# Half of an output projection by Strassen's seven products on two token blocks

## The chip, the cores and the metric

The kernel runs on one core of a Trainium2 chip. The metric is the device time of one launch in microseconds (us); lower is better. All of the profile's times are of one execution, counted from its first instruction.

The engines are named as the profile names them: PE (TensorE's products; PEld is its weight load), DVE (VectorE), ACT (ScalarE), POOL (GpSimd) and SP (which issues most transfers from HBM). Each engine works through its own list of instructions in order; an instruction that needs another engine's result or a free buffer waits for it at the head of its list, and everything behind it waits too.

## The reference

One layer of a hybrid encoder trunk is computed for 384 tokens: 256 of a prompt (two blocks of 128) and 128 of running streams (a third block). The part that matters here is the end of the mixer, on 2048 features:

```python
merged = (gates[:, :, 0] * br_pool + gates[:, :, 1] * br_ssd).astype(u.dtype)
out = merged @ p['w_out']                 # (384, 2048) @ (2048, 2048), float32
...
x = x + rmsnorm(m, p['g_mix_post'])
hdn = jnp.square(jax.nn.relu(rmsnorm(x, p['g_mlp_pre']) @ p['w_up'])) @ p['w_down']
x = x + rmsnorm(hdn, p['g_mlp_post'])
```

`m` is `out`. The norm of a token needs the sum of squares over all 2048 columns of its row of `out`, so nothing behind it can start for a token block before its last column block is there.

## The kernel before

Every large product is made in three passes at TensorE's full rate. An operand is split into a high part (ScalarE casts it to fp32r: `wh`, `mh`) and a low part (VectorE subtracts the high part: `wl`, `ml`), and the products high x high, high x low and low x high are added up in PSUM. So each weight tile of 128x1024 costs one ScalarE and one VectorE operation (`wsplit`, L77 and L78).

The stage before the change, `wo_units`, makes the output projection in four column blocks `nb` of 512 columns. A block has eight units `kp`; a unit loads one weight tile of 128x1024 (two k-steps of 128 features by 512 columns), splits it, and makes 2 k-steps x 3 token blocks x 3 passes = 18 products (L1082 to L1084) into three PSUM tiles `wo`, one for each token block. The stationary operand is the block's piece of `mh` or `ml` (the merged features, kept in SBUF in `ms_`), the moving one the weights. At the end of a block ScalarE squares each PSUM tile with a running sum (`wo_sums`, L1033) and VectorE multiplies it by the gain into `hm` (`wo_gain`, L1036).

Of the fourth block, the last three units are kept and worked off by token block (54 products in a row), so that the norm of token block 0 runs on VectorE and ScalarE while TensorE still multiplies for blocks 1 and 2: `wo_root` and `wo_scale` make the factor, `wo_out` (L1065) adds the scaled row to x. `transition` then turns x by TensorE transposes (`trm`, L1162) into the layout of the next product `pj_up`; filler products (`fill`, L1178 and L1180) on the first w_up tile run while it waits.

Order is set by hand. `flow` goes through a list of units: for unit i it first asks for the tile of unit i+4 (SP), then issues the products of unit i, then the splits of unit i+3 (three buffers each for `wh` and `wl`, so the split of unit i+3 waits for the products of unit i), then what follows the unit (`post`), then `work`, which takes small tasks that were put aside by `later` as far as a budget allows. Functions placed with `at` are called between two units and so stand at that place in every engine's list. `need(tag)` forces the tasks up to that tag.

The down projection further on already uses the seven-product form (`down_units`, `token_sums`, `merge`), with its token sums on VectorE and its results added up in HBM.

## Time and profile before

| | |
|---|---|
| runs | median 2798.02 us of 3 (2796.97 to 2801.68) |
| profiled execution | 2799.5 us, span from first to last instruction 2797.7 us |
| products of the output projection | 576, from 1627.7 to 1758.3 us |
| mean granted clock | 0.998 |

Rows of a profile are read so: line and engine, operation, output<-inputs by the program's names with buffer numbers left out, shape, xcount, then after the bar busy us, mean ns of one, and the engine's idle time just before them with what ended it. Matmuls overlap in the pipeline, so the time of one in a row is found from first to last start and the count, not from its duration. A window row gives, for a stretch of time, the busy time of PE, PEld, DVE, ACT and POOL with their counts, the granted clock, the share of the transfer engines' time and GB/s.

### The profile page before, as it was taken

The numbers are of one execution on the slowest core, as the hardware profiler recorded it, in microseconds if no ns is written. First come the engines' busy times: TensorE is split into PE (matmuls) and PEld (weight loads), VectorE is DVE, ScalarE is ACT, GpSimd is POOL, SyncE is SP. The second block draws the span as 40 slices with busy tenths as digits, with TensorE's granted clock in tenths as the row PEclk, the third lists the DMA queues.
The fourth block names the chain that finished last, engine by engine and source line by source line (L and its number), as shares of the span: only waits on it lengthen the run. The fifth ranks groups of instructions, "written<-read, shape, count | busy, mean of one in ns | idle before, by whom it ended". The sixth has DMA issues, their size and how long they took to land.

```text
span 2797.7 us, 40260 instructions
## 1 busy us (share of the span) xinstructions
PE 2784.7 (100%) x15964; PEld 2656.5 (95%) x15964; DVE 1766.9 (63%) x2217; ACT 1323.5 (47%) x2076; POOL 191.0 (7%) x295
## 2 busy tenths in 40 slices
PE   9999999999999999999999999999999999999998
PEld 9999999999999999999999988999999999999997
DVE  8774334567667767667633334666767667676766
ACT  6443223555555554554422223545555555555553
POOL 0000000000000000001000000000111111111111
PEclk9999999999999999999999999999999999999999
DMA  6444445556556556555744454445666566666656
GB/s 223 134 134 139 138 141 171 191 170 216 193 181 209 197 183 208 199 184 186 263 158 155 151 200 132 153 165 185 179 162 166 162 161 163 176 177 186 183 125 249
DMA packets 161468, 492.89 MB, mean 176 GB/s; under 512 B 20032, under 2 KB 43392, under 8 KB 156416
## 3 DMA queue, kind: packets, MB, share of 16 engines
q1 hardware_dynamic: 133008, 406.07, 43.1%
q0 software_dynamic: 28128, 84.24, 12.6%
q8 instruction: 125, 2.05, 0.3%
q14 instruction: 63, 0.52, 0.1%
q10 hardware_dynamic: 144, 0.01, 0.0%
HBM read 412.35 MB, written 77.89 MB: 175 GB/s over the span
## 4 chain that ended last, share of the span: by engine, by line
PE 94%; DVE 2%; DMA 1%; ACT 1%; issue 1%; SPq 0%; DVEq 0%; ACTq 0%
PE pj_up L162 6%; PE pj_up L163 6%; PE pj_up L164 6%; PE pj_x L162 4%; PE pj_x L163 4%; PE pj_x L164 4%; PE wd L1410 3%; PE pj_sp L162 3%; PE wd L1411 3%; PE wd L1412 3%; PE pj_sp L164 3%; PE pj_sp L163 3%; PE pj_z L163 3%; PE pj_z L164 3%; PE pj_z L162 3%; PE t L1412 2%
## 5 line engine op out<-in xcount | busy, mean ns | idle before, releaser
L162 PE MATMUL pj_up<-x1h,wh_up 128*128 128x384 f32 x992 | 334.6, 337 | 0.0
L163 PE MATMUL pj_up<-x1l,wh_up 128*128 128x384 f32 x992 | 333.7, 336 | 0.0
L164 PE MATMUL pj_up<-x1h,wl_up 128*128 128x384 f32 x992 | 333.7, 336 | 0.0
L162 PE MATMUL pj_x<-xgh,wh_x 128*128 128x384 f32 x768 | 257.6, 335 | 0.0
L164 PE MATMUL pj_x<-xgh,wl_x 128*128 128x384 f32 x768 | 256.9, 335 | 0.0
L163 PE MATMUL pj_x<-xgl,wh_x 128*128 128x384 f32 x768 | 256.9, 335 | 0.0
L78 DVE TENSOR_TENSOR wl_wd<-raw,wh_wd 128x1024 fp32r<-128x1024 f32 x168 | 201.8, 1223 | 62.7 <-ACT wh_wd L77 59.0
L77 ACT ACTIVATE wh_wd<-raw 128x1024 fp32r<-128x1024 f32 x168 | 174.2, 1053 | 84.5 <-PE pj_up L163 42.1
L162 PEld LDWEIGHTS pj_up<-x1h,wh_up 128*128 128x128 f32 x992 | 186.9, 188 | 4.5
L163 PEld LDWEIGHTS pj_up<-x1l,wh_up 128*128 128x128 f32 x992 | 186.9, 188 | 4.5
L164 PEld LDWEIGHTS pj_up<-x1h,wl_up 128*128 128x128 f32 x992 | 186.9, 188 | 0.0
L164 PE MATMUL pj_z<-xgh,wl_z 128*128 128x384 f32 x512 | 171.3, 335 | 0.0
L162 PE MATMUL pj_z<-xgh,wh_z 128*128 128x384 f32 x512 | 171.3, 335 | 0.0
L163 PE MATMUL pj_z<-xgl,wh_z 128*128 128x384 f32 x512 | 171.3, 335 | 0.0
L162 PE MATMUL pj_sp<-abh,wh_sp 128*128 128x384 f32 x512 | 171.2, 334 | 0.0
L164 PE MATMUL pj_sp<-abh,wl_sp 128*128 128x384 f32 x512 | 171.2, 334 | 0.0
L163 PE MATMUL pj_sp<-abl,wh_sp 128*128 128x384 f32 x512 | 171.2, 334 | 0.0
L78 DVE TENSOR_TENSOR wl_sp<-w_sp,wh_sp 128x1024 fp32r<-128x1024 f32 x64 | 78.4, 1226 | 110.7 <-ACT wh_sp L77 110.7
L162 PEld LDWEIGHTS pj_x<-xgh,wh_x 128*128 128x128 f32 x768 | 144.3, 188 | 0.0
L163 PEld LDWEIGHTS pj_x<-xgl,wh_x 128*128 128x128 f32 x768 | 144.3, 188 | 0.0
L164 PEld LDWEIGHTS pj_x<-xgh,wl_x 128*128 128x128 f32 x768 | 144.2, 188 | 0.0
L78 DVE TENSOR_TENSOR wl_x<-w_x,wh_x 128x1024 fp32r<-128x1024 f32 x72 | 87.4, 1221 | 81.3 <-ACT wh_x L77 81.3
(388 smaller groups left out, 7094.2 us busy)
## 6 DMA issues: line engine op xcount, KB each, us to landing
w_up<-w_up SPq DMA_DIRECT2D x126, 512.0 KB, 4.6
raw<-w_down SPq DMA_DIRECT2D x112, 512.0 KB, 7.1
w_x<-w_in SPq DMA_DIRECT2D x96, 512.0 KB, 4.0
w_z<-w_in SPq DMA_DIRECT2D x64, 512.0 KB, 4.5
w_sp<-w_ssd SPq DMA_DIRECT2D x64, 512.0 KB, 4.7
acc_scr<-ev POOLq DMA_DIRECT2D x126, 256.0 KB, 4.4
w_ga<-w_in SPq DMA_DIRECT2D x32, 512.0 KB, 3.4
w_pp<-w_pp SPq DMA_DIRECT2D x32, 512.0 KB, 3.4
```

Of the source, the lines that this page charges most:

```text
L77: s.activation(h, w, AF.Copy)
L78: v.tensor_tensor(l, w, h.bitcast(F32), ALU.subtract)
L162: te.matmul(out, wh, xh, start=first, stop=False)
L163: te.matmul(out, wh, xl, start=False, stop=False)
L164: return te.matmul(out, wl, xh, start=False, stop=last)
L1410: te.matmul(o, ah, wh[:, c], start=first, stop=False)
L1411: te.matmul(o, ah, wl[:, c], start=False, stop=False)
L1412: te.matmul(o, al, wh[:, c], start=False, stop=fin)
```

## The change

Columns 1024 to 2047 stay plain tiles (`wo_units(2)` and `wo_units(3)`, 16 units in all). Columns 0 to 1023 are made by `wo_pairs(c8)`, once for each half c8 of the 2048 features. For each half, the features (two groups of 512), the prompt's tokens (two blocks of 128) and the columns (two groups of 512) form a 2x2 by 2x2 block product, which takes seven products of token sums with weight sums; the third token block is multiplied plainly (tiles 7 and 8, named `wot`). Eight steps use one weight tile of 128x2048 each, in two units q; a unit makes 6 products for each of its one or two uses. Four weight tiles are loaded, and the other four steps use sums of weights that VectorE adds in place (`add`).

The token sums are made by GpSimd: `wo_tok_add` joins high and low parts of the merged features (four additions of 128x256), `wo_tok_diff` forms four sums in six operations, and `wo_tok_split` has ScalarE and VectorE split them. Results leave PSUM into nine SBUF tiles `wo_ac`: ScalarE copies those of the first half, VectorE adds those of the second. `wo_merge` puts seven operations on VectorE into the tasks, which make the four tiles of the two prompt blocks; their gain (6 products of 128x512) is made by GpSimd, in place, and their squares by ScalarE.

The order of the stage is a string. P is a plain unit; three digits are a paired unit (half c8, step j, part q); a and d are the additions and differences of tokens on GpSimd, c is their split, b is the squares and gain of the third block:

```python
    plain = wo_units(2) + wo_units(3)
    ones_ = wo_pairs(0), wo_pairs(1)
    order = "a00 d0 a01 d1 P P P c0 P 000 001 010 011 c1 a10 d0 a11 d1 020 021 030 031 P 040 041 P 050 051 P 060 061 070 071"
    order += " 100 101 c0 P 110 111 c1 120 121 130 131 P 140 141 P b0 150 b1 151 160 161 P 170 171"
```

Five plain units of the last block follow. The loads of x are put among the tasks; the first two w_up tiles are loaded when the paired units have ended (`wo_turn`) and split behind unit 6 of the last block instead of units 0 and 1; the sum over column blocks that the norm starts from (`wo_early`) comes after the merge. PSUM is given out as 2 + 2 + 4 banks instead of 4 + 4, and again as 4 + 4 in `transition`.

GpSimd's list at the start of the stage. Before, gains, x and w_up tiles are only loaded:

```order
L1028 DMA gpo0_15620<-g_mix_post 128x512
L1028 DMA gpo1_15622<-g_mix_post 128x512
L1021 DMA x1_15610<-x_tok 128x2048 x3
L1023 DMA w_x0_15618<-w_up 128x1024
L1023 DMA w_x1_15619<-w_up 128x1024
```

After the change:

```order
L1032 DMA gpo1_15632<-g_mix_post 128x512
L1157 ISA
L1157 TENSOR_TENSOR wo_t_15640<-mh0_13622,ml0_13623 128x256
L1157 TENSOR_TENSOR wo_t_15640<-mh1_13753,ml1_13754 128x256
L1157 TENSOR_TENSOR wo_t_15640<-mh4_14146,ml4_14147 128x256
L1157 TENSOR_TENSOR wo_t_15640<-mh5_14277,ml5_14278 128x256
L1171 TENSOR_TENSOR wo_sf0_15641<-wo_t_15640 128x256 x2
L1171 TENSOR_TENSOR wo_sf0_15641<-wo_sf0_15641 128x256
L1171 TENSOR_TENSOR wo_sf0_15641<-wo_t_15640 128x256 x2
L1171 TENSOR_TENSOR wo_sf0_15641<-wo_sf0_15641,wo_t_15640 128x256
```

The first ten additions stand behind the gains' loads and a row ISA; x's loads come behind the second ten.

VectorE's list at the end of a plain column block. Before, at the end of block 1 (`hm` are the gain products):

```order
L78 TENSOR_TENSOR wl_wo2_0_16003<-w_wo2_0_15934,wh_wo2_0_16002 128x1024
L78 TENSOR_TENSOR wl_wo2_1_16027<-w_wo2_1_15958,wh_wo2_1_16026 128x1024
L1036 TENSOR_TENSOR hm_15611<-wo1_0_15837,gpo1_15622 128x512
L1036 TENSOR_TENSOR hm_15611<-wo1_1_15838,gpo1_15622 128x512
L1036 TENSOR_TENSOR hm_15611<-wo1_2_15839,gpo1_15622 128x512
L78 TENSOR_TENSOR wl_wo2_2_16065<-w_wo2_2_15982,wh_wo2_2_16064 128x1024
```

After the change, at the end of block 2, which falls between the paired units 101 and 110 to 120 (`wl_wop1_2_0` is the low part of unit 120's weights, `wor` a weight tile, `wo_sl` a low part of token sums):

```order
L78 TENSOR_TENSOR wl_wop1_1_0_16127<-wor1_12_16079,wh_wop1_1_0_16126 128x1024
L1207 TENSOR_TENSOR wo_ac0_15617<-wor1_0_16095,wo_ac0_15617 128x512
L1176 TENSOR_TENSOR wo_sl_15644<-wo_sf0_15641,wo_sh_15643 128x4x256
L78 TENSOR_TENSOR wl_wop1_1_1_16153<-wor1_12_16079,wh_wop1_1_1_16152 128x1024
L1188 TENSOR_TENSOR wor1_11_16041<-wor1_11_16041,wor1_12_16079 128x2048
L1052 TENSOR_TENSOR hm0_15614<-wo2_0_15667,gpo2_15628 128x512
L1052 TENSOR_TENSOR hm1_15615<-wo2_1_15668,gpo2_15628 128x512
L1052 TENSOR_TENSOR hm2_15616<-wo2_2_15669,gpo2_15628 128x512
L78 TENSOR_TENSOR wl_wop1_2_0_16177<-wor1_21_16112,wh_wop1_2_0_16176 128x1024
```

Between two splits of weights there now stand a result from PSUM, a low part of token sums, an addition of weights and three gain products.

VectorE's list at the last unit. Before:

```order
L78 TENSOR_TENSOR wl_wo3_6_16373<-w_wo3_6_16306,wh_wo3_6_16372 128x1024
L78 TENSOR_TENSOR wl_wo3_7_16377<-w_wo3_7_16330,wh_wo3_7_16376 128x1024
L1036 TENSOR_TENSOR hm_15611<-wo3_0_16253,gpo3_16039 128x512
L1059 RECIPROCAL n2_10_16405<-n0_10_16400 128x1
L1060 TENSOR_SCALAR n1_10_16401<-n1_10_16401,n2_10_16405 128x1
```

After the change:

```order
L78 TENSOR_TENSOR wl_wo3_6_16506<-w_wo3_6_16430,wh_wo3_6_16505 128x1024
L1267 SCALAR_TENSOR_TENSOR wo_ac6_15623<-wo_ac6_15623,wo_ac4_15621 128x512
L1268 TENSOR_TENSOR wo_ac5_15622<-wo_ac5_15622,wo_ac4_15621 128x512
L78 TENSOR_TENSOR wl_wo3_7_16518<-w_wo3_7_16456,wh_wo3_7_16517 128x1024
L1269 SCALAR_TENSOR_TENSOR wo_ac2_15619<-wo_ac5_15622,wo_ac2_15619 128x512
L1062 TENSOR_TENSOR spre_16525<-st1_15626 128x3
L1063 TENSOR_TENSOR spre_16525<-spre_16525,st1_15626 128x3
L1064 TENSOR_SCALAR sneg_16526<-spre_16525 128x3
L1065 TENSOR_SCALAR spre_16525<-spre_16525 128x3
L1141 TENSOR_TENSOR wl_x0_16451<-w_x0_16448,wh_x0_16450 128x1024
L1141 TENSOR_TENSOR wl_x1_16453<-w_x1_16449,wh_x1_16452 128x1024
L1052 TENSOR_TENSOR wo_ac0_15617<-wo3_0_16268,gpo3_16166 128x512
```

The last merge, the small sums and the low parts of the two w_up tiles stand between the last split and the first gain product of the norm.

The diff, without the order string above, the loads and the PSUM lines that only follow from it:

```diff
+    def hm(b, nb):
+        return wo["ac"][(1, 2, 3, 6, 7, 8)[b * 2 + nb]] if nb < 2 else wo["hm"][b] if nb == 2 else wo["ac"][(0, 4, 5)[b]]
...
     def wo_gain(nb, b):
-        v.tensor_tensor(wo["hm"][:, b, blk(nb)], wo["o", nb][b], wo["gpo", nb], ALU.mult)
+        if nb > 1:
+            v.tensor_tensor(hm(b, nb), wo["o", nb][b], wo["gpo", nb], ALU.mult)
+        else:
+            gp.tensor_tensor(hm(b, nb), hm(b, nb), wo["gpo", nb], ALU.mult)
...
-            if nb == 3 and kp in (0, 1):
-                w = wo["raw"][kp]
-                h, l = wo["first"][kp]
-                s.activation(h, w, AF.Copy)
-                v.tensor_tensor(l, w, h.bitcast(F32), ALU.subtract)
+            if nb == 3 and kp == 5:
+                need("wo_early")
+            if nb == 3 and kp == 6:
+                for w, (h, l) in zip(wo["raw"], wo["first"]):
+                    s.activation(h, w, AF.Copy)
+                    v.tensor_tensor(l, w, h.bitcast(F32), ALU.subtract)
...
+    def wo_tok_add(c8, j):
+        for i, k in enumerate((2 * j, 2 * j + 1, 4 + 2 * j, 5 + 2 * j)):
+            h, l = (x[:, :TP].bitcast(F32) for x in ms_[c8 * 8 + k])
+            gp.tensor_tensor(wo["t32"][:, i, :], h, l, ALU.add)
+
+    def wo_tok_diff(j):
...
+        ):
+            gp.tensor_tensor(o, x, y, op)
+
+    def wo_tok_split(j):
+        ks = slice(2 * j, 2 * j + 2)
+        s.activation(wo["sh"][:, :, ks, :], wo["sf"][j], AF.Copy)
+        v.tensor_tensor(wo["sl"][:, :, ks, :], wo["sf"][j], wo["sh"][:, :, ks, :].bitcast(F32), ALU.subtract)
+
+    def wo_pairs(c8):
...
+        def add(d, n):
+            v.tensor_tensor(raw[d], raw[d], raw[n], ALU.add)
+
+        steps = [
+            ("11", True, [(0, tok(0, 0)), (7, tok(0, 2))], nothing),
+            ("12", True, [(8, tok(0, 2))], lambda: add("11", "12")),
+            ("21", True, [(1, tok(4, 0)), (7, tok(4, 2))], nothing),
+            ("22", True, [(2, sums(3)), (8, tok(4, 2))], lambda: add("12", "22")),
+            ("11", False, [(4, sums(0))], lambda: add("22", "11")),
+            ("12", False, [(6, sums(2))], lambda: add("21", "22")),
+            ("22", False, [(5, sums(1))], nothing),
+            ("21", False, [(3, tok(4, 1))], nothing),
+        ]
...
+        def evict(r, o):
+            a = wo["ac"][r]
+            if c8 == 0:
+                s.copy(a, o)
+            else:
+                v.tensor_tensor(a, o, a, ALU.add)
...
+    def wo_merge():
+        a1, a2, a3, a4, a5, a6, a7 = wo["ac"][:7]
+        tt, stt = v.tensor_tensor, v.scalar_tensor_tensor
+        parts = [
+            lambda: tt(a2, a1, a2, ALU.add),
...
+        ]
+        for i, b, nb in ((2, 0, 0), (5, 1, 0), (7, 1, 1), (10, 0, 1)):
+            parts.insert(i, lambda nb=nb, b=b: wo_part(nb, b))
+        for i, f in enumerate(parts):
+            later(0.6, None, f)
+        later(0.6, "wo_early", wo_early)
...
-    for nb in range(4):
-        items += wo_units(nb)
...
+    at(wo_turn)
+    at(wo_merge)
+    items += plain
```

More of the change, by code (lines that the diff above doesn't have):

```diff
@@ L1012, in wo_open @@
         wo["x1"] = xp.tile([P, 3, DM], F32, name="x1")
-        wo["hm"] = xp.tile([P, 3, DM], F32, name="hm")
+        wo["hm"] = [xp.tile([P, 512], F32, name=f"hm{i}") for i in range(3)]
+        wo["ac"] = [xp.tile([P, 512], F32, name=f"wo_ac{i}") for i in range(9)]
         wo["st"] = xp.tile([P, 3, 4], F32, name="st1")
         wo["st2"] = xp.tile([P, 3, 4], F32, name="st2")
-        wo["first"] = [[xp.tile([P, 1024], F32R, name=f"w{n}_x{i}") for n in "hl"] for i in range(2)]
-        wo["raw"] = [xp.tile([P, 1024], F32, name=f"w_x{i}") for i in range(2)]
@@ L1018, in wo_open @@
-        for nb in range(2):
+        for nb in (2, 0, 1):
             gain_load(nb)
         for b in range(3):
-            gp.dma_start(wo["x1"][:, b, :], io["x_tok"][b])
+            later(0.0, None, lambda b=b: gp.dma_start(wo["x1"][:, b, :], io["x_tok"][b]))
+        wo["pairs"] = ExitStack()
+        sp_ = wo["pairs"].enter_context(tc.tile_pool(name="wop", bufs=1, reuse_waits="tile"))
+        wo["rawp"] = wo["pairs"].enter_context(tc.tile_pool(name="wor", bufs=4, reuse_waits="tile"))
+        wo["t32"] = sp_.tile([P, 4, TP], F32, name="wo_t")
@@ new lines, in wo_open, with gain_load, wo_turn @@
+        wo["sf"] = [sp_.tile([P, 4, 2, P], F32, name=f"wo_sf{i}") for i in range(2)]
+        wo["sh"], wo["sl"] = (sp_.tile([P, 4, 4, P], F32R, name=f"wo_s{n}") for n in "hl")
+        for f in wo["late"]:
+            f()
+    def gain_load(nb):
+        g = wo["gpo", nb] = wo["p2"].tile([P, 512], F32, tag="gpo", name=f"gpo{nb}", bufs=3)
+        gp.dma_start(g, io["g_mix_post"][blk(nb)].partition_broadcast(P))
+    def wo_turn():
+        wo["pairs"].close()
+        xp = wo["hold"].enter_context(tc.tile_pool(name="x1p3", bufs=1, reuse_waits="tile"))
+        wo["raw"] = [xp.tile([P, 1024], F32, name=f"w_x{i}") for i in range(2)]
+        wo["first"] = [[xp.tile([P, 1024], F32R, name=f"w{n}_x{i}") for n in "hl"] for i in range(2)]
```

104 lines of the change are left out of this document (89 added, 15 removed).

## The prediction

> **What bounds the kernel now.** I read the totals first, then the waits of the stage, its products, its windows, its groups, and its last microseconds in order of time.
>
> ```profile
> span 2797.7 us, 40260 instructions
> ...
> PE 2784.7 (100%) x15964; PEld 2656.5 (95%) x15964; DVE 1766.9 (63%) x2217; ACT 1323.5 (47%) x2076; POOL 191.0 (7%) x295
> ```
>
> TensorE is busy for 2784.7 of 2797.7 us. What counts is how many products it has and whether anybody makes it wait. From 1610 to 1800 us the view of TensorE's waits has three rows:
>
> ```profile
> PE trm L1162 <- issue: 0.6, 1, 0.6
> PE pj_up L1201 <- DVE x1l L1170: 0.5, 1, 0.5
> PE trm L1162 <- DVE x L1065: 0.3, 1, 0.3
> ```
>
> All three lie behind the output projection, in the turn of x to the next layer's layout; inside the projection TensorE never waits. The products, from the view of the tile wo (count, shortest/median/longest ns, first and last start), and the windows (busy time of TensorE, weight load, DVE, ACT, POOL; granted clock; DMA):
>
> ```profile
> L1082 PE MATMUL wo<-wh_wo,mh x192: 387/389/390, 1627.7 to 1757.6; 128*128 128x512 f32 x192
> L1083 PE MATMUL wo<-wl_wo,mh x192: 388/390/397, 1627.9 to 1757.9; 128*128 128x512 f32 x192
> L1084 PE MATMUL wo<-wh_wo,ml x192: 388/390/398, 1628.2 to 1758.1; 128*128 128x512 f32 x192
> ```
>
> ```profile
> 1627.70:1758.30 130.60, 130.60 (x578) 108.10 (x577) 53.13 (x62) 46.08 (x68) 2.22 (x5) 1.00 0.49 164
> 1758.30:1764.50 6.20, 4.89 (x30) 3.88 (x29) 5.18 (x13) 3.76 (x12) 0.00 (x0) 1.00 0.00 1
> 1764.50:1768.00 3.50, 3.50 (x14) 3.40 (x13) 1.95 (x5) 0.00 (x0) 0.00 (x0) 0.51 0.00 0
> ```
>
> The 576 products start from 1627.7 to 1758.1, so one takes 130.4/575 = 0.227 us; the 390 ns is its length in the pipeline. VectorE is busy 53 of 131 us, ScalarE 46, GpSimd 2. A plain tile (18 products) lasts 4.08 us. Behind the projection the clock is granted at 0.51 for 3.5 us.
>
> **Products (the gain).** Two of the four column blocks of 512 need 3 token blocks x 16 k-steps x 2 x 3 products = 288 now. The new form has, for each half of the features, 11 uses (2+1+2+2+1+1+1+1 over the eight steps) of 4 k-steps with 3 products, 132; twice that is 264. So 24 x 0.227 = **-5.4 us**. This is all that the change can take off: 0.19%.
>
> **VectorE and ScalarE in the stage.** Prices, from the groups of 1627.7 to 1758.3 us and, for operations that only the later down projection has, of the rest of the run:
>
> ```profile
> L78 DVE TENSOR_TENSOR wl_wo<-w_wo,wh_wo 128x1024 fp32r<-128x1024 f32 x30 | 36.8, 1226 | 69.0 <-ACT wh_wo L77 69.0
> L1036 DVE TENSOR_TENSOR hm<-wo,gpo 128x512 f32<-128x512 f32 x11 | 7.6, 689 | 6.2 <-ACT q L1033 6.2
> ```
>
> ```profile
> L1358 DVE TENSOR_TENSOR raw<-raw,raw 128x2048 f32<-128x2048 f32 x56 | 127.9, 2284 | 0.0
> L1308 DVE TENSOR_TENSOR sl<-sf,sh 128x1024 fp32r<-128x1024 f32 x14 | 17.2, 1226 | 15.8 <-ACT sh L1307 15.8
> L1461 DVE TENSOR_TENSOR ac<-wd,ac 128x512 f32<-128x512 f32 x12 | 7.7, 682 | 0.0
> ```
>
> ```profile
> L77 ACT ACTIVATE wh_wo<-w_wo 128x1024 fp32r<-128x1024 f32 x30 | 31.8, 1059 | 73.1 <-PE wo L1084 71.6 <-issue 1.5
> L1033 ACT ACTIVATE q<-wo 128x512 f32<-128x512 f32 x11 | 6.6, 599 | 9.7 <-PE wo L1084 9.7
> L1033 ACT ACTIVATION_READ_ACCUMULATOR q<-wo 128x1 f32 x11 | 2.1, 194 | 0.0
> ```
>
> Sixteen more weight splits, 8 additions of weights, 4 low parts of token sums, 9 additions from PSUM and 7 merges put 16 x 1.226 + 8 x 2.284 + 4 x 1.226 + 16 x 0.69 = 53.8 us on VectorE and take away 6 gain products of 0.69. In the stretch of the paired units themselves (264 products and 7 plain tiles of 18: 390 x 0.227 = 88.5 us) VectorE has 38 splits, 8 additions, 3 low parts and 11 operations from PSUM: 46.6 + 18.3 + 3.7 + 7.6 = 76.2 us, 86%. So 12.3 us are spare on the whole, but no longer beside each unit: a unit of one use lasts 6 x 0.227 = 1.36 us, and only two units are split ahead. ScalarE (splits of 1.06 us, copies of the first half's results) has less and is no bound.
>
> The place with least cover is the end of the third plain column block, ahead of unit 120 (the order of VectorE there is shown above). TensorE then has units 110 and 111, 12 products, 2.72 us. ScalarE squares the last block (0.60 + 0.19), splits the weights (1.06), VectorE makes the low part (1.23): 3.1 us, so TensorE waits 0.4. I allow as much again for like places: **+0.8**.
>
> **The tail.** What ran early now stands in front of the norm: the two splits of the first w_up tiles, the last merge, the four sums of squares. The rows of VectorE, ScalarE and TensorE from 1747 to 1763 us, in order of time (start, duration):
>
> ```profile
> 1747.37 1.23 DVE L78 TENSOR_TENSOR wl_wo<-w_wo,wh_wo 128x1024 fp32r<-128x1024 f32 x1 [2.86 <-ACT wh_wo L77]
> 1751.08 0.69 DVE L1036 TENSOR_TENSOR hm<-wo,gpo 128x512 f32<-128x512 f32 x1 [2.48 <-ACT q L1033]
> 1752.68 0.16 DVE L1059 RECIPROCAL n<-n 128x1 f32<-128x1 f32 x1 [0.92 <-ACT n L1052]
> 1753.46 2.08 DVE L1065 SCALAR_TENSOR_TENSOR x<-hm,n,x 128x512 f32<-128x512 f32 x3
> ...
> 1757.48 2.08 DVE L1065 SCALAR_TENSOR_TENSOR x<-hm,n,x 128x512 f32<-128x512 f32 x3
> ...
> 1761.50 0.75 DVE L1065 SCALAR_TENSOR_TENSOR x<-hm,n,x 128x512 f32<-128x512 f32 x1
> ```
>
> ```profile
> 1751.06 1.28 ACT L1052 ACT_TABLE_LOAD   x1
> ```
>
> ```profile
> 1758.32 1.04 PE L1162 MATMUL trm<-cst,x 128*128 128x128 f32 x8
> 1762.36 0.63 PE L1162 MATMUL trm<-cst,x 128*128 128x128 f32 x4 [0.63 <-issue]
> ```
>
> Call 0 the start of the last 54 products (1758.3 - 54 x 0.227 = 1746.1). Now VectorE ends the last split at 2.5, idles, and ends the last x row that the turn waits for at 1762.25, that is 16.15. After the change: last split 2.5, merge 0.69 to 3.2, ScalarE's square to 4.0, VectorE's four small sums to 4.8; ScalarE's two casts run from 4.0 to 6.0, VectorE's two low parts (1.14 apart) to 7.4, its gain to 8.1. ScalarE: square to 6.8, table load to 8.1, roots to 8.4. From there the old chain: 0.78 to the first x row (9.2), three of them 2.0, gain and row 1.25, next root 0.77: the first row of block 1 is done at 13.95 where TensorE is free at 12.25; three rows, gain, row, root and the last row end at 18.0. So **+1.85** against 16.15. Only about 2.2 us of the 6 us of moved work show, since VectorE used to idle there.
>
> **GpSimd.** It gets 40 additions of 128x256 and 6 gain products of 128x512, behind a row ISA. No run here has an operation of GpSimd with inputs; its nearest rows and its last free moment:
>
> ```profile
> L499 POOL MEMSET bst<- 128x1024 f32 x1 | 1.0, 973 | 0.0
> ...
> L338 POOL MEMSET pbuf<- 128x15 f32 x2 | 0.2, 110 | 31.7 <-DVE xgl L256 31.7
> ```
>
> ```profile
> 1625.05 1.11 POOL L1028 DMA_DIRECT2D gpo<-g_mix_post  x2 [261.15 <-PE pj_sp L164]
> ```
>
> A column costs (973 - 110)/1009 = 0.86 ns to write. An addition of 256 columns is then 0.10 + 0.22 = 0.32 us if its two reads are hidden, 0.76 if reads and write go one after another. I take the middle, 0.54 (1.0 for 512 columns, 1.41 at most). ScalarE must read the first sums by 1643.4: four plain tiles end at 1644.0, unit 000 at 1646.75, and the cast of the sums (1.06) and the split behind it (1.06 + 1.23) stand ahead of unit 001. GpSimd has 1626.7 to 1643.4, 16.7 us, for ten additions (5.4, at most 7.6): cost 0, and 9 us cover the ISA row. The second ten are wanted at 1654: covered too.
>
> Whether GpSimd and VectorE hold each other up when both read SBUF no row tells. Bounds: nothing; or every GpSimd operation that meets VectorE delays it by its whole length. About 30 additions and 2 gain products fall into the stretch of 88.5 us, 18.2 us, of which 86% meet VectorE: 76.2 + 15.7 = 91.9, +3.4 over TensorE's 88.5; in the tail the four gain products stand between the merges, in front of the last split, where one of 1.0 delays TensorE directly: +1.3 with the merge that it also pushes. I take +2 of the 3.4, since operations that meet are half over on average, and the 1.3: **+3.3**. The Trainium skill's page "SBUF — State Buffer", section "Who interferes with whom", speaks against the change here: a VectorE instruction with two SBUF inputs and a GpSimd instruction that reads SBUF exclude each other, and the second waits for all of the first. By that rule the 3.4 stand in place of my 2, and the sum below would be +2.0 instead of +0.6; no run here shows it yet.
>
> **Transfers.** SP issues as many bytes; the paired halves are asked for four units ahead, 5.5 us at the tightest (unit 020 asked for at 1644.0, split at 1649.5). The weights' tiles land so (shortest, median, longest), while x's three transfers, now behind GpSimd's sums, take long:
>
> ```profile
> DMA to landing us min/median/max: 3.3/3.4/8.6
> ```
>
> ```profile
> x<-x_tok POOLq DMA_DIRECT2D x3, 1024.0 KB, 11.5
> ```
>
> At 3.4 us they are covered; 8.6 beside x's transfers would cost up to 3 us once. I take 0 and keep the 3 for the range. The first w_up tiles are wanted some 15 us after their issue: 0. PSUM's two banks for results come free one step ahead: 0.
>
> **Sum:** -5.4 + 0.8 + 1.85 + 3.3 = **+0.6 us**, on a profiled execution of 2799.5 us (span 2797.7). The median of the runs, 2798.02, is 1.5 below it; I set the sum on the median: **2798.6**. The runs spread over 2796.97 to 2801.68, so about 0.2% (5.6 us) is what can be told from no change.
>
> **Rivals.** (1) GpSimd and VectorE do not meet: -5.4 + 0.8 + 1.85 = -2.8, 2795.2. For it: the additions from PSUM and most units leave VectorE gaps; against it: 86% load. (2) Slower: GpSimd holds VectorE up, at 0.76 and 1.41 us. 0.86 x (30 x 0.76 + 2 x 1.41) = 22.0 and 76.2 + 22.0 - 88.5 = +9.7, tail +2: -2.8 + 11.7 = +8.9, 2806.9. It decides against the change (+5.6) from about 0.65 us an addition. (3) GpSimd's first sums come late: ScalarE stands at their cast with all splits behind it, and each microsecond beyond the 9 of cover is one of TensorE; at 15 us for the ISA row +6, 2804.6. The Trainium skill's page "GPSIMD Engine Reference", section 2.1, gives about 6 us for loading a kernel's code at first use, which would be covered. (4) The gain stays whole: moved work hides and the 3.5 us at clock 0.51 fall away (half of it, -1.7): 2798.0 - 5.4 - 1.7 = 2790.9.
>
> **Chances.** Forecast 0.48, (1) 0.22, (2) 0.18, (3) 0.07, (4) 0.05. Faster by over 0.2% is (4) alone, 0.05; slower by over 0.2% is (2), (3) and a little of the forecast, 0.28; within it 0.67. The range leaves out (4) and the far part of (2) and (3): 2793.5 to 2807.0.
>
> **What would show it.** TensorE's count falls by 24; the waits of TensorE name wl_wop, the low halves of the paired tiles, for 1 to 4 us in all, and wl_wo of the last tile for about 1; the first turn of x starts 1.5 us or more after the last product; GpSimd's additions show 0.5 to 0.6 us. VectorE's low parts (1226 ns) unchanged beside running additions would speak for rival 1. ScalarE waiting for the sums at their cast would speak for rival 3. A wait on w_out2's transfers, or a second stretch at half clock, would make the prediction wrong in a way not counted here.

## The result, and the profile after

| | before | after |
|---|---|---|
| median of the runs | 2798.39 us (12 runs, 2796.66 to 2802.30) | 2805.04 us (12 runs, 2803.99 to 2808.36) |
| ratio | 1 | 1.0024, 95% interval 1.0016 to 1.0032 |
| profiled execution | 2799.5 us, span 2797.7 us | 2804.69 us, span 2802.6 us |

The change costs 6.65 us, just over the 0.2% that can be told from no change. The forecast was 2798.6 us; 2805.04 lies inside the range (2793.5 to 2807.0), but 6.4 us above the forecast and on the side that had 0.28 of the chance.

The totals of the page after show that the products did go: 15940 instead of 15964. VectorE has 64 us more to do and GpSimd 62.

```profile
PE 2781.5 (99%) x15940; PEld 2650.2 (95%) x15940; DVE 1831.3 (65%) x2255; ACT 1349.2 (48%) x2105; POOL 252.8 (9%) x341
```

The waits of TensorE from 1610 to 1810 us (total, times, longest) have grown from three rows, 1.4 us in all, to five, 9.7 us:

```profile
PE wor L1243 <- DVE wl_wop L78: 4.1, 3, 2.3
PE trm L1320 <- DVE x L1083: 2.6, 2, 2.3
PE wo L1101 <- DVE wl_wo L78: 1.7, 2, 1.0
PE trm L1320 <- issue: 0.7, 1, 0.7
PE pj_up L1359 <- DVE x1l L1328: 0.6, 1, 0.6
```

One by one, in order of time (start, duration, the product that waited, how long and for whom):

```profile
1653.48 0.50 PE L1243 MATMUL wor<-wl_wop,mh 128*128 128x512 f32 x1 [2.28 <-DVE wl_wop L78]
1674.01 0.50 PE L1101 MATMUL wo<-wl_wo,mh 128*128 128x512 f32 x1 [0.74 <-DVE wl_wo L78]
1703.94 0.50 PE L1243 MATMUL wor<-wl_wop,mh 128*128 128x512 f32 x1 [0.66 <-DVE wl_wop L78]
1730.27 0.50 PE L1243 MATMUL wor<-wl_wop,wo_sh 128*128 128x512 f32 x1 [1.19 <-DVE wl_wop L78]
1752.54 0.50 PE L1101 MATMUL wo<-wl_wo,mh 128*128 128x512 f32 x1 [0.99 <-DVE wl_wo L78]
1764.51 0.33 PE L1320 MATMUL trm<-cst,x 128*128 128x128 f32 x1 [2.27 <-DVE x L1083]
```

To see where the time went, I cut both profiled executions at the same three events: from the first product of the projection to the first turn of x, from there to the first product of `pj_up`, and on to its first product of line L162, where the turn is over. The windows of before (busy time of TensorE, weight load, VectorE, ScalarE, GpSimd; granted clock; transfers):

```profile
1627.71:1758.32 130.61, 130.61 (x577) 108.09 (x577) 53.16 (x62) 46.08 (x68) 2.21 (x5) 1.00 0.49 164
1758.32:1763.11 4.79, 4.03 (x27) 3.36 (x25) 3.77 (x9) 3.04 (x10) 0.00 (x0) 1.00 0.00 2
1763.11:1786.93 23.82, 22.98 (x132) 21.92 (x133) 15.49 (x28) 15.20 (x34) 0.54 (x1) 0.93 0.46 177
```

And of after, with a fourth row for 3.45 us behind the first long wait:

```profile
1626.30:1761.97 135.67, 129.66 (x553) 104.18 (x553) 113.40 (x94) 69.88 (x93) 59.49 (x47) 0.99 0.44 153
1761.97:1769.33 7.36, 4.23 (x28) 3.31 (x26) 6.16 (x15) 4.49 (x14) 0.00 (x0) 1.00 0.00 0
1769.33:1791.75 22.42, 21.54 (x132) 20.32 (x133) 15.50 (x28) 15.19 (x34) 0.60 (x1) 1.00 0.47 186
...
1653.55:1657.00 3.45, 3.45 (x9) 2.73 (x10) 3.45 (x3) 0.00 (x0) 3.45 (x3) 0.55 0.00 0
```

The projection is 5.06 us longer in spite of 24 products fewer, the turn 2.57 us longer, the piece behind it 1.40 us shorter: there the stretch at half clock that before has is gone, and it stands in the projection now, behind the wait of 2.28 us. Together +6.23 us. The span grew by 4.9 only because the untouched work ahead took 1.41 us less in this execution (first product at 1626.30 instead of 1627.71); execution to execution this start moved between 1625.7 and 1628.8 us in the kernels below. So the stretch between the cuts, 159.22 us before and 165.45 after, is the sharper measure, and I give it for each kernel beside its median.

The groups of VectorE in the projection show what the waits came from. Its low parts took 1226 ns before, its additions of weights 2284; the operations with an input in PSUM (`wo_ac<-wor`) kept their length:

```profile
L78 DVE TENSOR_TENSOR wl_wop<-wor,wh_wop 128x1024 fp32r<-128x1024 f32 x32 | 46.2, 1458 | 14.7 <-ACT wh_wop L77 11.9 <-DMA w_wo<-w_out 2.8
L1188 DVE TENSOR_TENSOR wor<-wor,wor 128x2048 f32<-128x2048 f32 x8 | 21.0, 2625 | 0.0
L1176 DVE TENSOR_TENSOR wo_sl<-wo_sf,wo_sh 128x1024 fp32r<-128x1024 f32 x4 | 5.9, 1486 | 0.0
L1207 DVE TENSOR_TENSOR wo_ac<-wor,wo_ac 128x512 f32<-128x512 f32 x7 | 4.8, 682 | 0.0
```

GpSimd's additions (shortest/median/longest ns) take 0.73 us when nothing is in their way and up to 2.78 us, 2.05 us more, while VectorE's addition of weights takes 2.28:

```profile
L1157 POOL TENSOR_TENSOR wo_t<-mh,ml x16: 725/752/2781, 1621.7 to 1665.2; 128x256 f32<-128x256 f32 x16
L1171 POOL TENSOR_TENSOR wo_sf<-wo_t x16: 731/1608/2782, 1624.6 to 1672.8; 128x256 f32<-128x256 f32 x16
```

VectorE in order of time around the first wait: it stands still nowhere between 1643.95 and 1658.4, but two low parts take 5.07 us instead of 2.36 (two of 1226 ns, their starts 1.14 apart) and the next ones 3.42:

```profile
1643.95 5.07 DVE L78 TENSOR_TENSOR wl_wop<-wor,wh_wop 128x1024 fp32r<-128x1024 f32 x2 [2.82 <-DMA w_wo<-w_out]
1648.94 2.83 DVE L1188 TENSOR_TENSOR wor<-wor,wor 128x2048 f32<-128x2048 f32 x1
1651.69 3.42 DVE L78 TENSOR_TENSOR wl_wop<-wor,wh_wop 128x1024 fp32r<-128x1024 f32 x2
1655.03 1.75 DVE L1176 TENSOR_TENSOR wo_sl<-wo_sf,wo_sh 128x1024 fp32r<-128x1024 f32 x1
```

VectorE's lengthening comes in steps. In the stretch of the paired units, 14 of its operations are 0.52 to 0.55 us longer than with nothing beside them (a low part 1.75 instead of 1.22, an addition of weights 2.83 instead of 2.28), the first low part is longer by four such steps (3.39 us), and two operations beside GpSimd's gains are longer by 1.10 and 1.14 us: the addition of 3.38 us at 1724.55 and a low part of 2.36 us at 1727.86. The 18 steps, for 20 additions, and the two gains make 11.9 us. GpSimd in the same time:

```profile
1644.10 3.82 POOL L1157 TENSOR_TENSOR wo_t<-mh,ml 128x256 f32<-128x256 f32 x4
1648.01 4.34 POOL L1171 TENSOR_TENSOR wo_sf<-wo_t 128x256 f32<-128x256 f32 x2
1652.42 1.59 POOL L1171 TENSOR_TENSOR wo_sf<-wo_sf 128x256 f32<-128x256 f32 x1
1653.99 3.38 POOL L1171 TENSOR_TENSOR wo_sf<-wo_t 128x256 f32<-128x256 f32 x2
```

### The profile page after: what moved, and what is told of

It reads as the page before. It is cut to its first block, busy times and chain, and to the rows that moved or that the text cites. A ratio compares the mean times of both kernels' runs of the same rounds, so it can differ in the third digit from the quotient of the medians.

```text
span 2802.6 us, 40341 instructions
## 1 busy us (share of the span) xinstructions
PE 2781.5 (99%) x15940; PEld 2650.2 (95%) x15940; DVE 1831.3 (65%) x2255; ACT 1349.2 (48%) x2105; POOL 252.8 (9%) x341
## 3 DMA queue, kind: packets, MB, share of 16 engines
q8 instruction: 125, 2.05, 0.3%
## 4 chain that ended last, share of the span: by engine, by line
PE 93%; DVE 3%; ACT 1%; issue 1%; DMA 1%; SPq 0%; DVEq 0%; ACTq 0%
PE pj_up L162 6%; PE pj_up L164 6%; PE pj_up L163 6%; PE pj_x L164 4%; PE pj_x L163 4%; PE pj_x L162 4%; PE wd L1568 3%; PE wd L1570 3%; PE pj_sp L162 3%; PE wd L1569 3%; PE pj_sp L164 3%; PE pj_sp L163 3%; PE pj_z L162 3%; PE pj_z L164 3%; PE pj_z L163 3%; PE t L1568 2%
## 5 line engine op out<-in xcount | busy, mean ns | idle before, releaser
L162 PE MATMUL pj_up<-x1h,wh_up 128*128 128x384 f32 x992 | 334.2, 337 | 0.0
L162 PE MATMUL pj_x<-xgh,wh_x 128*128 128x384 f32 x768 | 257.2, 335 | 0.0
L162 PEld LDWEIGHTS pj_up<-x1h,wh_up 128*128 128x128 f32 x992 | 186.5, 188 | 4.5
L162 PE MATMUL pj_z<-xgh,wh_z 128*128 128x384 f32 x512 | 171.1, 334 | 0.0
L162 PE MATMUL pj_sp<-abh,wh_sp 128*128 128x384 f32 x512 | 171.0, 334 | 0.0
L1536 POOL DMA_DIRECT2D acc_scr<-ev x108 | 93.9, 937 | 666.5 <-ACT ev L1532 651.4
L162 PEld LDWEIGHTS pj_x<-xgh,wh_x 128*128 128x128 f32 x768 | 144.2, 188 | 0.0
```

What stands on the lines that cost most here:

```text
L162: te.matmul(out, wh, xh, start=first, stop=False)
L1536: gp.dma_start(acc_scr[p][r], e, accum_op=ALU.add)
```

## The experiments

Theory A: GpSimd's reads hold VectorE up where VectorE is full, and that is most of the loss. Theory B: VectorE's own load and the moved tail make it, and GpSimd does no harm. All results, each against runs of the kernel before on the same chip:

| kernel | median us | before us | ratio (95%) | stretch between the cuts us |
|---|---|---|---|---|
| after | 2805.04 | 2798.39 | 1.0024 (1.0016 to 1.0032) | 165.45 |
| e1_write_only | 2801.08 | 2797.99 | 1.0011 (1.0003 to 1.0020) | 161.35 |
| e2_gains_vector | 2802.41 | 2797.99 | 1.0017 (1.0008 to 1.0026) | 162.18 |
| e3_sums_twice | 2806.21 | 2797.99 | 1.0031 (1.0020 to 1.0043) | 168.46 |
| e4_no_low_up | 2804.08 | 2797.99 | 1.0023 (1.0014 to 1.0032) | 163.94 |
| e5_early_sums | 2802.78 | 2798.32 | 1.0018 (1.0009 to 1.0027) | 162.18 |
| e6_plain_places | 2804.48 | 2798.32 | 1.0022 (1.0012 to 1.0032) | 163.84 |
| e7_all | 2795.78 | 2798.32 | 0.9994 (0.9984 to 1.0003) | 156.13 |
| e8_six_last | 2794.09 | 2797.60 | 0.9987 (0.9978 to 0.9996) | 155.36 |
| e9_sums_vector | 2796.53 | 2797.60 | 1.0000 (0.9991 to 1.0009) | 156.83 |
| e10_plain_tokens | 2792.92 | 2797.61 | 0.9985 (0.9976 to 0.9995) | 153.55 |

The medians of the kernel before differ by 0.8 us between the chips (2797.60 to 2798.39), so less than that says nothing. The last column is of one profiled execution each, and holds no, one or two stretches at half clock of 1.7 us loss (before, after, e1 and e8 one each, e3 two, the others none).

### GpSimd writes and does not read

```diff
-            h, l = (x[:, :TP].bitcast(F32) for x in ms_[c8 * 8 + k])
-            gp.tensor_tensor(wo["t32"][:, i, :], h, l, ALU.add)
+            gp.memset(wo["t32"][:, i, :], 0.0)
...
-            gp.tensor_tensor(o, x, y, op)
+            gp.memset(o, 0.0)
```

> GpSimd's 40 additions of 128x256 are replaced by 40 writes of a constant into the same tiles at the same places (the token sums are left out; gains stay on GpSimd). Theory A (the loss in the paired stretch comes from GpSimd's reads, which hold VectorE up): VectorE's low parts of paired tiles go back to about 1226 ns, the waits of 2.28 and 0.74 us on wl_wop and wl_wo near 1653 and 1674 us vanish with the stretch at half clock behind the first, and the time is 3 us or more below the changed kernel's 2805.0: 2800 to 2802. Theory B (VectorE's own load and the thin covers make the waits, GpSimd does no harm): the waits stay, 2804 to 2806. Theory C (any GpSimd access to SBUF holds VectorE up, a write too): low parts stay longer than 1.3 us beside the writes, and the gain is about half of A's, since a write is shorter than an addition.

Measured: 2801.08 us, 4.0 below the changed kernel. The waits near 1653 and 1674 us are gone, the other three of the projection stand as they were. VectorE's low parts and GpSimd's writes in this kernel:

```profile
L78 DVE TENSOR_TENSOR wl_wop<-wor,wh_wop 128x1024 fp32r<-128x1024 f32 x32 | 39.9, 1257 | 19.5 <-ACT wh_wop L77 19.5
L1175 DVE TENSOR_TENSOR wo_sl<-wo_sf,wo_sh 128x1024 fp32r<-128x1024 f32 x4 | 4.9, 1217 | 0.0
...
L1170 POOL MEMSET wo_sf<- 128x256 f32 x24 | 6.7, 310 | 21.5 <-DVE wo_sl L1175 21.0
```

Theory A holds for the sums, theory B falls there, and so does C: no operation of VectorE is longer beside GpSimd's writes. A write is also shorter than an addition (0.31 against 0.73 us), but if it held VectorE in proportion, steps of some 0.2 us (estimated from the 0.53) would show, and beside the writes every low part takes 1.21 to 1.23 us. The mean is 1257 and not 1220 ns because of one low part of 2361 ns beside a gain product, which GpSimd still makes here. The rule that the prediction weighed (the Trainium skill, "SBUF — State Buffer", "Who interferes with whom": a VectorE instruction with two inputs in SBUF and a GpSimd instruction that reads SBUF exclude each other) agrees with this trace: 1458 ns beside additions, 1257 beside writes, and no change in the operations with an input in PSUM.

### The gains on VectorE

```diff
-            gp.tensor_tensor(hm(b, nb), hm(b, nb), wo["gpo", nb], ALU.mult)
+            v.tensor_tensor(hm(b, nb), hm(b, nb), wo["gpo", nb], ALU.mult)
```

> The six gain products of the merged tiles go to VectorE; the token sums stay on GpSimd. Theory A: VectorE gets 6 x 0.69 = 4.1 us of work, but its additions and merges that lasted 3.38, 1.68 and 1.78 us beside GpSimd's gains go back to 2.28 and 0.69 us, and its splits likewise, together about 4.6 us; the wait of 1.19 us near 1730 us and that of 0.99 us at the last split shrink by half or more: 2803 to 2804.5. Theory B: VectorE has 4.1 us more to do in the two thinnest places and nothing less: 2806 to 2808, with a longer wait at the last split and at the first turn of x.

Measured: 2802.41 us, 2.6 below the changed kernel, more than expected; the profiled execution has no stretch at half clock, which is 1.7 us of its 3.3 between the cuts. The wait of 1.19 us is gone, the one at the last split is 0.71 instead of 0.99, the one at the first turn 1.41 instead of 2.27. The 0.74 us near 1674 are two waits here (0.56 and 0.60), as in e3, e4 and e6, which have no half-clock stretch just ahead of that place:

```profile
PE wor L1243 <- DVE wl_wop L78: 3.0, 2, 2.3
PE wo L1101 <- DVE wl_wo L78: 1.9, 3, 0.7
PE trm L1320 <- DVE x L1083: 1.7, 2, 1.4
```

So six products that look free on an idle engine cost more there than the 4.1 us that VectorE needs to make them itself. Of the operations from 1715 us to the turn that both kernels have, one addition of weights was 1.10 us longer beside GpSimd's gains, two merges 1.09 and 0.98, one of the small sums 1.00 and the 14 splits together 1.35: 5.5 us. The first of them in the changed kernel:

```profile
1723.74 2.04 POOL L1054 TENSOR_TENSOR wo_ac<-wo_ac,gpo 128x512 f32<-128x512 f32 x1 [20.12 <-ACT q L1048]
1724.55 3.38 DVE L1188 TENSOR_TENSOR wor<-wor,wor 128x2048 f32<-128x2048 f32 x1
```

### The second half's sums twice

```diff
-            gp.tensor_tensor(wo["t32"][:, i, :], h, l, ALU.add)
+            for _ in range(1 + c8):
+                gp.tensor_tensor(wo["t32"][:, i, :], h, l, ALU.add)
...
-            gp.tensor_tensor(o, x, y, op)
+            for _ in range(1 + c8 * (x is not o)):
+                gp.tensor_tensor(o, x, y, op)
```

> Of the second half's 20 token sums on GpSimd, the 16 that can be repeated without changing their result are issued twice (about 16 x 1.3 us more, so GpSimd works to about 1696 us instead of 1676; the sums are wanted at 1702). Theory A: VectorE is held up for another 20 us in the stretch, 0.5 us for each addition that it meets, of which part is spare time: waits of TensorE on wl_wop grow by 1 to 4 us, 2806 to 2809. Theory B: no change, 2804 to 2806.

Measured: 2806.21 us, at the lower end of A's range and hardly outside B's. The trace tells them apart: GpSimd works to 1704 us, and the wait at unit 120, 0.66 us in the changed kernel with GpSimd idle, is now

```profile
1704.01 0.71 PE L1245 MATMUL wor<-wl_wop,mh 128*128 128x512 f32 x1 [2.01 <-DVE wl_wop L78]
```

That is 1.35 us more for additions which change nothing else, at a place that they did not touch before. (The first wait, at instructions that are the same, is 1.64 us in this execution and 2.28 in the changed kernel's: so much it varies by itself.) Sixteen additions thus cost about 1.3 us where plain tiles stand between the paired units, less than the 3.0 us (2.28 and 0.74) of the twenty beside the first paired units.

### The tail without the low parts of w_up

```diff
                     s.activation(h, w, AF.Copy)
-                    v.tensor_tensor(l, w, h.bitcast(F32), ALU.subtract)
```

> The low parts of the first two w_up tiles are left out of VectorE's list in front of the norm (GpSimd writes zeros there when their transfers are issued), so VectorE has 2.36 us less between the last merge and the first gain product. If the moved splits make the tail late, the wait at the first turn of x (2.27 us, 1.85 forecast for all that was moved) falls to under 1 us, 2803 to 2804. If the last merge, GpSimd's gains and ScalarE's squares set the tail, the wait stays above 1.5 us and the time within 0.7 us of 2805.0.

Measured: 2804.08 us; the wait at the first turn is 1.46 us instead of 2.27, between the two cases. The low parts are 0.8 us of it, not all. ScalarE's list of the changed kernel shows what else stands ahead of the norm, though how much of the rest it makes was not measured. Token block 0's last product starts at 1753.57 us (its 18 products end 36 of 0.227 us ahead of the last one, at 1761.73), but its square stands behind the square of the last merge and two casts for w_up:

```profile
1753.18 0.63 ACT L1048 ACTIVATE q<-wo_ac 128x512 f32<-128x512 f32 x1 [2.19 <-DVE wo_ac L1269]
1753.71 0.19 ACT L1048 ACTIVATION_READ_ACCUMULATOR q<-wo_ac 128x1 f32 x1
1753.81 2.00 ACT L1140 ACTIVATE wh_x<-w_x 128x1024 fp32r<-128x1024 f32 x2
1755.71 0.57 ACT L1048 ACTIVATE q<-wo 128x512 f32<-128x512 f32 x1
```

### The same sums, earlier

The first ten additions go into the stage before, the other thirty ahead of the paired units (the tiles `wo_t` and `wo_sf0` into a pool that is open there):

```diff
-    order = "a00 d0 a01 d1 P P P c0 P 000 001 010 011 c1 a10 d0 a11 d1 020 021 030 031 P 040 041 P 050 051 P 060 061 070 071"
+    order = "a01 d1 c0 P a10 d0 c1 P a11 d1 P P 000 001 010 011 020 021 030 031 P 040 041 P 050 051 P 060 061 070 071"
...
+        if n == 8:
+            at(wo_tok_add, 0, 0)
+            at(wo_tok_diff, 0)
```

> The same 40 additions on GpSimd, only earlier: the first ten in the middle of the stage before, the other thirty ahead of the paired units (order a01 d1 c0 P a10 d0 c1 P a11 d1 P P 000 ...), where VectorE has spare time; gains and tail as in the changed kernel. If what costs is that GpSimd's reads meet VectorE where VectorE is full, the waits of 2.28 and 0.74 us vanish and the time is that of the kernel whose additions were only writes (2801.1), within 1 us. If the additions cost wherever they stand (GpSimd and VectorE meet in the plain units too), the waits move to the plain units and the time stays within 1 us of 2805.0.

Measured: 2802.78 us, 2.3 below the changed kernel, between the two cases. The wait of 0.74 us is gone. The one of 2.28 is 1.56, about the 1.64 of e3, since the last ten sums do not end before the paired units begin (at about 1642.6 us) but at 1659.0. One of them, right behind that wait:

```profile
1653.35 1.60 POOL L1016 TENSOR_TENSOR wo_sf<-wo_sf 128x256 f32<-128x256 f32 x1
```

28 of the 40 additions are done before the paired units begin, and no wait of TensorE names a low part there; the wait that went is theirs. Of the 3.3 us between the cuts, 1.7 are the half-clock stretch, which this execution has not.

### Other places for the plain tiles

```diff
-    order += " 100 101 c0 P 110 111 c1 120 121 130 131 P 140 141 P b0 150 b1 151 160 161 P 170 171"
+    order += " 100 101 c0 110 P 111 c1 120 121 130 131 P 140 141 P b0 150 b1 151 P 160 161 170 171"
```

> Only the places of plain tiles among the second half's paired units change (100 101 c0 110 P 111 c1 ... 141 P b0 150 b1 151 P 160 161 170 171), so that the unit with the end of the third plain block is followed by more products; GpSimd as in the changed kernel. If the waits of 0.66 us at unit 120 and of 1.19 us near 1730 us are a matter of thin cover on VectorE, both shrink to under 0.3 us and the time falls by 1 to 2 us: 2803 to 2804. If they belong to the work as a whole (VectorE 86% busy), they appear at another unit and the time stays within 0.7 us of 2805.0.

Measured: 2804.48 us, which can't be told from 2805.04. The wait of 0.66 us at unit 120 is gone, so that one was thin cover; the 1.19 us stay to the hundredth, only at a plain unit (1729.82 us). With the gains on VectorE (e2) they vanish at the old places. So they belong to GpSimd's gains; of the two cases expected, thin cover holds for the smaller wait alone.

### All three together

Early sums, gains on VectorE (each one merge later than its square, so that VectorE need not wait for ScalarE), and other places in both halves:

```diff
+    order = "a01 d1 c0 P a10 d0 c1 P a11 d1 P P 000 001 010 P 011 020 021 030 031 040 P 041 P 050 051 060 061 070 071"
+    order += " 100 101 c0 110 P 111 c1 120 121 130 131 P 140 141 P b0 150 b1 151 P 160 161 170 171"
...
+        sq, gain = (lambda nb, b: lambda: wo_sums(nb, b)), (lambda nb, b: lambda: wo_gain(nb, b))
+        a, c, d, e, f, g, h = parts
+        parts = [a, c, sq(0, 0), d, e, gain(0, 0), sq(0, 1), f, gain(0, 1), sq(1, 1), g, h, sq(1, 0), gain(1, 1)]
```

> Early sums on GpSimd, gains on VectorE one merge later than their squares, and other places for the plain tiles in both halves. If the three causes (GpSimd's reads where VectorE is full, gains on GpSimd in the tail, thin covers) are the whole loss in the projection, TensorE has less than 0.5 us of waits between its first product of the projection and its last, the gain of 5.4 us is whole up to the tail, where the first turn of x waits 1.4 us (as with the gains on VectorE): span 2.5 to 4 us shorter than before's, 2794 to 2796, faster than the kernel before. If there is another loss (a wait on a transfer, VectorE's load as such), it shows as a wait of TensorE and the time is 2797 or more. A stretch at half clock more or less than in before moves either by 1.7 us.

Measured: 2795.78 us, as expected; the interval of its ratio still holds 1. All waits of TensorE from 1610 to 1810 us:

```profile
PE trm L1327 <- DVE x L1107: 2.3, 2, 1.9
PE trm L1327 <- issue: 0.7, 1, 0.7
PE pj_up L1366 <- DVE x1l L1335: 0.6, 1, 0.6
```

In the projection the view lists none. The three causes were all of the waits that it had listed.

### One more plain tile behind the pairs

```diff
-    order += " 100 101 c0 110 P 111 c1 120 121 130 131 P 140 141 P b0 150 b1 151 P 160 161 170 171"
+    order += " 100 101 c0 110 P 111 c1 120 121 130 131 P 140 141 150 b1 P 151 160 161 170 b0 171"
```

> As the kernel with early sums, gains on VectorE and other places, but six plain units instead of five behind the last paired unit, so that the seven merges, four gains and the w_up splits have one more tile of 18 products (4.1 us) beside them. If the 1.92 us at the first turn of x are VectorE's and ScalarE's load in front of the norm (ScalarE squares token block 0 at 2.2 us after its last product instead of 0.1), the wait falls below 0.6 us and the time by 1 to 2 us: 2793.5 to 2795, faster than before by 3 to 5 us. If the wait comes from the order of the norm's own operations, it stays near 1.9 us and the time at 2795.8. If the stretch, one plain tile poorer, becomes too full for VectorE, TensorE waits on wl_wop again.

Measured: 2794.09 us, 3.5 faster than the kernel before, and the interval is below 1. The wait for the x row is 0.2 us, the turn lasts 4.98 us against 4.79 before:

```profile
1625.95:1752.64 126.69, 126.69 (x554) 103.13 (x553) 108.20 (x105) 70.86 (x96) 33.77 (x31) 1.00 0.47 164
1752.64:1757.62 4.98, 4.12 (x27) 3.31 (x26) 3.96 (x10) 3.23 (x12) 0.00 (x0) 1.00 0.00 0
```

So the long wait at the turn was load in front of the norm, and one tile of 18 products covers it. This version beats both kernels.

### The sums on VectorE

```diff
-            gp.tensor_tensor(wo["t32"][:, i, :], h, l, ALU.add)
+            v.tensor_tensor(wo["t32"][:, i, :], h, l, ALU.add)
...
-            gp.tensor_tensor(o, x, y, op)
+            v.tensor_tensor(o, x, y, op)
```

> The same with the 40 token sums on VectorE at the same places. GpSimd then reads nothing beside VectorE, but VectorE gets 40 additions of 128x256, of some 0.35 us each (half of a 128x512 one of 0.69), in bursts of ten: 3.5 us in a row ahead of the paired units, 14 us in all. If the exclusion costs VectorE as much as the additions themselves (0.5 us for each that meets one of its operations), the low parts go back to 1.23 us and the time stays within 1 us of the sums on GpSimd. If GpSimd's help is worth its price, VectorE's bursts delay a split and TensorE waits 1 to 3 us more on wl_wo in the plain units ahead of the pairs: 2795 to 2798.

Measured: 2796.53 us, 2.4 slower than the same places with GpSimd. The low parts are back to their old length, and TensorE waits 1.62 us on wl_wo at 1640 and 0.45 on wl_wop at 1645 us:

```profile
L78 DVE TENSOR_TENSOR wl_wop<-wor,wh_wop 128x1024 fp32r<-128x1024 f32 x32 | 38.5, 1220 | 9.8 <-ACT wh_wop L77 9.7
...
L1002 DVE TENSOR_TENSOR wo_t<-mh,ml 128x256 f32<-128x256 f32 x12 | 4.3, 416 | 0.0
```

At these places GpSimd's help is worth its price, though not because it saves VectorE work: an addition of 0.42 us is taken off VectorE's bursts, and a hold-up costs it 0.53. With GpSimd TensorE has neither of these waits, so the hold-ups fall into VectorE's spare time.

### Products with a token sum as stationary operand

Where the view of waits lists nothing, the projection still lasts 126.69 us, 1.5 more than 552 products at the 0.2268 us of before (130.61/576).

```diff
-        sums = lambda i: lambda k: [wo["sh"][:, i, k, :], wo["sl"][:, i, k, :]]
+        sums = lambda i: tok(4 * (i & 1), i >> 1)
```

> As the kernel with six plain units last, but the 96 products whose stationary operand is a token sum (tiles wo_sh, wo_sl) take a plain piece of the tokens (mh, ml) in its place; the sums are made and split as before and not used (so the results of these products are not the reference's). In that kernel the projection has no wait of TensorE and yet lasts 126.7 us for 552 products, 0.2295 us each against 0.2268 before; products with wo_sh or wo_sl start 0.2335 us after the one ahead, others 0.2268 to 0.229. If the operand's tile is the cause, their step falls to 0.229 or less and the projection lasts 126.0 to 126.3 us (time 0.4 to 0.7 us shorter, which the runs can't tell). If the cause is the place (units of one use, other engines at work there), the step stays at 0.2335 and the projection at 126.7 us.

Measured: the projection lasts 126.14 us, 0.55 less, and the 96 products step by 0.227 on average instead of 0.233:

```profile
1625.86:1752.00 126.14, 126.09 (x554) 103.11 (x553) 108.43 (x105) 70.94 (x96) 33.85 (x31) 1.00 0.47 165
```

The tile is the cause of that part. What it is about these tiles (place, layout, values) was not tried. Of the other 0.9 us, 0.8 are seven steps of 0.27 to 0.43 us at the starts of four units, which the view of waits does not list, since the product ahead, 0.39 us long in the pipeline, has only just ended. They too are waits for low parts: at each of the four, the product that first reads a low part starts 0.05 to 0.08 us after VectorE has ended it. The longest step is that of the product at 1654.89 us; the low part that it reads is the first of these two, 1.75 us long:

```profile
1653.08 3.44 DVE L78 TENSOR_TENSOR wl_wop<-wor,wh_wop 128x1024 fp32r<-128x1024 f32 x2
```

## Why the prediction was right or wrong

The signs and places of the terms were right; the sum was 5.6 us too low, because one term was less than half of what it came to and two were missing. That the time still lies in the range is owed to the room that the range had for rivals 2 and 3, not to the sum. In the profiled execution, against before:

| term | predicted us | measured us | from |
|---|---|---|---|
| 24 products fewer | -5.4 | -5.4 | count 15964 to 15940 |
| products start further apart | 0 | +1.5 | 126.69 us where the view lists no wait (e8), less 552 x 0.2268 |
| thin cover ahead of unit 120 | +0.8 | +0.7 | wait of 0.66; moved away in e6 |
| GpSimd beside VectorE in the stretch | +2.0 | +4.2 | waits of 2.28 and 0.74 (e1), 1.19 (e2) |
| what the waits cost beyond the view's figure | 0 | +1.5 | the ten product steps at the five waits are 7.35 us too long, the view names 5.86 |
| tail: moved work, gains on GpSimd | +3.15 | +3.6 | last split 0.99, turn +2.57 |
| half-clock stretch | 0 | +1.6, then -1.4 | nine product steps behind the first wait (1.7 by the clock); moved from behind the turn into the projection |
| sum | +0.6 | +6.3 | +6.23 between the cuts, the rest is rounding |

The fifth row: at the wait of 2.28 us the product that waited starts 2.67 us behind the one ahead, and the next one 0.34 us behind it, instead of 0.227 each.

**Products.** Right in count. "This is all that the change can take off" was right, but not all came: the new ones step wider, 0.55 us of it by the tiles of their stationary operand.

**VectorE and ScalarE in the stretch.** Right: the wait came at the place named, ahead of unit 120, and its 0.66 us lay between the 0.4 worked out for it and the 0.8 with the allowance for like places.

**GpSimd: the step that failed.** The mechanism was named, and the rule that spoke against the change was weighed, but the step from hold-ups to waits was wrong: I set 86% load and the hold-ups of the whole stretch against its length, as if spare time anywhere could pay. The hold-ups themselves were overestimated: 30 additions at 0.54 and two gains at 1.0, 86% of which meet VectorE, are 15.7 us, and 18 steps of 0.53 us and two of 1.1, 11.9 us, were measured. By my own sum, 76.2 + 11.9 - 88.5, that costs nothing, and TensorE waited 4.2 us. Splits run only two units ahead, so 4.3 us of hold-up within 11 us (the rows from 1643.95 on: 2.71, 0.55 and 1.06) become a wait even where the stretch as a whole has room. So that the average gave a cost at all, 2 or 3.4, came from the number of additions counted too high. The price of GpSimd's own work was also off, 0.73 us for an undisturbed addition and about 1.3 for a gain product instead of 0.54 and 1.0; but what VectorE loses to an addition, 0.53 us, is close to what I had taken.

**Tail.** 3.15 forecast, 3.6 measured. The chain was right in its parts (last merge, square, two casts, two low parts, gain). The last split's own 0.99 us of waiting, with the gains on GpSimd ahead of it, was in the 1.3; e4 and e2 give 0.8 us to the low parts and 0.9 to the gains at the turn.

**Transfers and PSUM.** Right at 0: no wait of TensorE names either. VectorE's idle 2.82 us ahead of 1643.95 is put down to a transfer, but stands behind ScalarE's cast of the same tile, which waits for a buffer.

**Rivals.** Rival 1 fell (e1). Rival 2 was nearest in time, 2806.9 against 2805.04, and right in that GpSimd holds VectorE up and that this decides against the change. Its sum was luck: it had 22.0 us of hold-up on average where 11.9 were measured, 30 additions of 0.76 us where 20 met the stretch (the first began at 1621.7 us, not 1626.7, so half of the 40 were done before the pairs began) and each held VectorE 0.53 us. Rival 3 fell: GpSimd's first addition began at 1621.7 us right behind the gains' loads, and ScalarE never waited for a sum. Rival 4's half-clock stretch did fall away behind the turn, only to stand elsewhere; a second such stretch was listed as not counted, and the wait of 2.28 us was followed by one.

## What to carry to other kernels

An idle engine is not free help: price its work by what it takes from the engine that it shares with, and put it where that engine has spare time within the few units that run ahead, not within the stage on average. Here an addition on GpSimd held VectorE 0.53 us, more than the 0.42 us that VectorE needs to make it, and a gain product 1.1 us against 0.69: such help pays only where the hold-up falls into spare time. Where no row shows a price, ask from which price the sign changes; but here even the right price, put into an average, would have given no loss. A gain of 5.4 us of products was real, but 3.5 us of it came only after every piece of moved work had its own cover.

## What the runs showed that was not expected

Stretches of 3.4 us at half clock, 1.7 us lost each, came behind waits of TensorE of 2.28 us (after), 2.01 us (e3) or some 0.6 us (before, at the turn), and stayed away behind waits of the same 2.28 to 2.29 us in e2, e4 and e6. The Trainium skill's page "TensorE: Matmul & The Clock Gate" (section "Part 1: The HAM clock gate (the "warmup" mystery)") gives a free-running window of 3413 ns, which agrees with their length, and half rate after an idle window of that length; no wait here was that long, so by these traces such a stretch can begin without one. Part of what decides is how a wait lies in time.

In each trace the changes of the granted clock lie whole multiples of 3.413 us apart (in the changed kernel the first stretch begins 1648.64 us, 483 such slices, behind the first change and the next change comes 334 slices after its end). The wait of 2.28 us falls into one slice in the changed kernel, and that slice is busy for 1.13 of 3.41 us; in e2 a wait of 2.29 us lies across two. The windows, the first of the changed kernel, the others of e2:

```profile
1650.47:1653.88 3.41, 1.13 (x6) 0.62 (x5) 3.41 (x3) 2.14 (x3) 3.33 (x2) 1.00 0.47 199
```

```profile
1648.69:1652.10 3.41, 1.94 (x9) 1.28 (x7) 3.41 (x2) 3.05 (x4) 3.33 (x3) 1.00 0.76 320
1652.11:1655.52 3.41, 2.60 (x11) 2.15 (x12) 3.41 (x3) 0.00 (x0) 3.41 (x3) 1.00 0.00 0
```

Within the projections of all these kernels, half clock followed the two slices with the least work, 1.13 us (changed kernel) and 1.40 us (e3), and no slice with 1.77 us (e3) or more. At the turn, where transposes are mixed in, busy time does not decide: 2.11 us were followed by half clock in the kernel before, 1.70 us in e5 were not. What does was not settled.

A product whose stationary operand lies in the token-sum tiles starts 0.233 us behind the one ahead (mean of the 96 in e8), the others 0.227 to 0.228 where no low part was late (means for the tiles `wo`, `wor` and `wot`).
